# A bias table filled by copies on GpSimd instead of one-hot products on TensorE

## The chip, the cores and the metric

The kernel runs on one core of one Trainium2 chip. The metric is the device time of one execution in microseconds (us). A core has five engines with a queue of instructions each: TensorE (PE in the profile; its weight loads, PEld, overlap the products), VectorE (DVE), ScalarE (ACT), GpSimd (POOL) and SyncE (SP), which here issues nearly all transfers. An engine takes its queue in order; engines wait for each other and for transfers through semaphores.

## The reference

It is a two-layer encoder over 256 tokens of width 1024, in float32. Each layer has a mixer and a gated MLP with a width-3 convolution. The mixer projects the normed input to a pooling branch, to queries, keys and values of 12 heads, and to two gates. The heads form three groups with (window, dilation) of (128, 1), (512, 4) and (2048, 16). What matters here is the bias on the logits:

```
half = window // (2 * dilation)
buckets = _t5_buckets(dilation * np.arange(-half, half + 1))
bias = rel_bias[buckets][:, hs].T            # rel_bias: (32 buckets, 12 heads)
logits = logits + bias[None, :, None, :]
logits = where(valid, logits, NEG_INF)
```

So the bias of a query and a key depends on their distance, through one of 32 buckets, and on the head. Keys outside the window, or off the dilation's grid, are masked. Both layers use the same table.

## The kernel before

Tokens are kept as two interleaved halves (even and odd, `t`), 128 each, on the partitions. Float32 products are made of three reduced products of a high and a low part (`wh`, `wl`, made of each weight by a ScalarE cast, L177 or L185, and a VectorE subtraction, L178 or L186).

The class `Weights` streams all weights in order. `load` (L109, transfer at L117) fetches raw tiles of 1 MB through three buffers; each raw tile is cut into two pieces; a piece is split into `wh` and `wl` some three pieces ahead of its use (`get`, L194, with `LOOK` 3 and five buffers). A projection (`proj`, L479) takes one piece: eight products with 512 columns at L475 and eight with 256 columns at L477.

Layer 0 begins with the values of the first head group (`begin_values_of_x`, L582), in an order written out by hand, and the other two groups (`first_values`, L704, products at L734). After that come `load_params` (L339), the bias table, and then the eight projections of the pooling branch (L793 to L801), two for each window, then queries and keys, with the attention steps put among them.

Outside the part ordered by hand, the framework plans the order of each engine's instructions itself: it runs the program against its own costs and puts an instruction into its engine's queue when its inputs are expected to be there, in program order where several are ready. Transfers on SP are therefore not all in program order. `tc.issue_after(W.behind[1].ins)` puts what is traced inside it behind one VectorE instruction, for the instructions on that same engine only.

The bias table: for each of five kinds (distance parity and dilation) and each of 4 heads of a group there are 256 places along the distance. `_bias_table` (L54) is made on the host: rows 0 to 31 are one-hot over the buckets, row 32 holds the mask (NEG where the distance is invalid, 0 elsewhere). `load_bias` (L354) fetches it (33 x 1280) into the tag `ybig` and `rel_bias` with a row of ones below it, and splits `rel_bias` into `rh` and `rl`; ScalarE casts the table into the tag `m2`. `build_bias` (L368) is a generator: for each kind it makes two products (L374) into PSUM and a VectorE copy (L378) into `fsb`, in the tag `q1`; it is moved on by one kind before each pooling projection (L800). After the fifth, `fsb` (4 x 1280) goes to DRAM (`fd`, L383), from there 128 times over to `sk` (2.5 MB, L385), and five skewed reads (L390) make `bt`, in which the place of a query and a key is aligned. `scores` adds `bt` to the logits (L878).

The tags are single buffers with several users in turn. `m2` first holds the pieces of the first value weights, later `po2` (L943). `q1` holds `xul` (the low part of the raw input) through the values, later the queries `q`. `ybig` holds pieces of the first values, later `pl2`.

Of the kernel before, what the change touches and what calls it, by code (L numbers as in the profile page):

```python
# [10 lines left out]
F32 = mybir.dt.float32  # L11
F32R = mybir.dt.float32r
# [4 lines left out]
P = 128  # L17
# [5 lines left out]
HPG = 4  # L23
NG = 3
NH = HPG * NG
# [8 lines left out]
NT = 5  # L34
# [10 lines left out]
def _buckets(rel):  # L45
    n = -rel
    ret = (n < 0).astype(np.int32) * 16
    n = np.abs(n)
    large = 8 + (np.log(np.maximum(n, 1) / 8) / np.log(1024 / 8) * 8).astype(np.int32)
    large = np.minimum(large, 15)  # L50
    return (ret + np.where(n < 8, n, large)).astype(np.int32)


def _bias_table():  # L54

    t = np.zeros((33, NT, 256), np.float32)
    delta = np.arange(255) - 127
    for n, (e, dil) in enumerate(
        ((2 * delta, 1), (2 * delta + 1, 1), (2 * delta - 1, 1), (2 * delta, 4), (2 * delta, 16))
    ):  # L60
        valid = (e % dil == 0) & (np.abs(e) <= 64 * dil)
        b = _buckets(e)
        j = np.nonzero(valid)[0]
        t[b[j], n, j] = 1.0
        t[32, n, np.nonzero(~valid)[0]] = NEG
        t[32, n, 255] = NEG
    return t.reshape(33, NT * 256)


def _edge_table():  # L70
# [134 lines left out]
def encoder(ctx, tc, x, w_in, w_pool, pool_scale, w_a, w_b, w_o, norm1, norm2, w_up, conv_w,  # L205
            conv_b, w_down, rel_bias, norm_f, onehot, edges, out):
    nc = tc.nc
    const = ctx.enter_context(tc.tile_pool(name="const", bufs=1))
    wpool = ctx.enter_context(tc.tile_pool(name="weights", bufs=1))
    big = ctx.enter_context(tc.tile_pool(name="big", bufs=1))  # L210
    sm = ctx.enter_context(tc.tile_pool(name="small", bufs=2))
    acc = ctx.enter_context(tc.tile_pool(name="acc", bufs=4, space=bass.MemoryType.PSUM))
# [6 lines left out]
    def cols(w, c0):  # L219

        src = w[:, c0 : c0 + 256].rearrange("(k p) c -> p k c", p=P)
        return W.add(
            src, (8, 256), [((lambda t, j=j: t[:, :, j * P : (j + 1) * P]), (8, P)) for j in (0, 1)]
        )
# [10 lines left out]
    for l in range(DEPTH):  # L235
        for g in range(NG):
            c0 = C_V + g * 512
            slots = (("m2", 0, 2), ("m2", 1, 2), ("ybig",), ("at2",)) if g == 0 else ()
            for j in range(2):
                tag = "k1" if l == 0 and g == 1 and j == 0 else None  # L240
# [34 lines left out]
        for f in range(0, NF, 2):  # L275
            a = cols(w_up[l], f * P) if f >= ENTRY else []
            g = cols(w_up[l], DFF + f * P)
# [7 lines left out]
    h = const.tile([P, 2, D], F32, name="h")  # L285
# [53 lines left out]
    def load_params():  # L339

        nc.sync.dma_start(out=edge.rearrange("p a b -> p (a b)"), in_=edges[0].partition_broadcast(P))
        for l in range(DEPTH):
            rowst = sm.tile([96, P], F32, tag="s", name="prow")
            nc.sync.dma_start(out=rowst[0:66, :], in_=conv_w[l].rearrange("w (f p) -> (w f) p", p=P))
            nc.sync.dma_start(out=rowst[66:88, :], in_=conv_b[l].rearrange("(f p) -> f p", p=P))
            nc.sync.dma_start(out=rowst[88:96, :], in_=pool_scale[l].rearrange("(f p) -> f p", p=P))
            pt = mmp.tile([P, 512], F32, tag="mm", name="prm_ps")
            nc.tensor.transpose(pt[:, :96], rowst, ident[:96, :96])
            nc.vector.tensor_copy(prm[:, l, :], pt[:, :96])
            nc.vector.tensor_scalar_mul(hps[:, l, :], prm[:, l, 88:96], 0.5)  # L350

    bt = const.tile([P, HPG, NT * P], F32, name="bt")

    def load_bias():  # L354
        oh = big.tile([33, NT * 256], F32, tag="ybig", name="onehot_sb")
        nc.sync.dma_start(out=oh, in_=onehot)
        rb = sm.tile([33, NH], F32, tag="rb", bufs=1, name="rb")
        nc.vector.memset(rb, 1.0)
        nc.sync.dma_start(out=rb[0:32, :], in_=rel_bias)
        rh = sm.tile([33, NH], F32R, tag="ms", name="rh")  # L360
        rl = sm.tile([33, NH], F32R, tag="ms", name="rl")
        nc.vector.tensor_copy(rh, rb)
        nc.vector.tensor_sub(out=rl, in0=rb, in1=rh.bitcast(F32))
        ohr = big.tile([33, NT * 256], F32R, tag="m2", name="onehot_r")
        nc.scalar.copy(out=ohr, in_=oh)
        return rh, rl, ohr

    def build_bias(rh, rl, ohr):  # L368

        fsb = big.tile([HPG, NT * 256], F32, tag="q1", name="fsb")  # L370
        for n, g in enumerate((0, 0, 0, 1, 2)):
            ps = acc.tile([P, 512], F32, tag="acc", name="f_ps")
            for j, r in enumerate((rh, rl)):
                nc.tensor.matmul(  # L374
                    ps[:HPG, :256], r[:, g * HPG : (g + 1) * HPG], ohr[:, n * 256 : (n + 1) * 256],
                    start=(j == 0), stop=(j == 1),
                )
            nc.vector.tensor_copy(fsb[:, n * 256 : (n + 1) * 256], ps[:HPG, :256])  # L378
            yield

        n = HPG * NT * 256
        fd = dram.tile([1, n], F32, name="fd")
        nc.sync.dma_start(out=fd[0].rearrange("(h e) -> h e", h=HPG), in_=fsb)  # L383
        sk = dram.tile([P, n + 1], F32, name="sk")
        nc.sync.dma_start(out=sk[:, 0:n], in_=fd[0].partition_broadcast(P))  # L385
        for blk, kind in enumerate((2, 0, 1, 3, 4)):
            src = bass.AP(
                sk.tensor, sk.offset + kind * 256 + 127, [[n, P], [NT * 256, HPG], [1, P]]
            )
            nc.sync.dma_start(out=bt[:, :, blk * P : (blk + 1) * P], in_=src)  # L390
        yield

    def bias_of(t, hh):

# [96 lines left out]
    def in_order(a):  # L491

        return a.rearrange("p (m t) -> p t m", t=2)
# [70 lines left out]
    def v_tile():  # L564
        return acc.tile([P, 512], F32, tag="acc", name="v_ps")
# [176 lines left out]
    for l in range(DEPTH):  # L742
# [25 lines left out]
        else:  # L768
            for g in range(NG):
                held = begun[0] if g == 0 else [W.get() for _ in range(4)]  # L770
                for t in range(2):
                    if g + t == 0:
                        ps = begun[1]
                    else:
                        ps = v_tile()
# [6 lines left out]
        if l == 0:  # L782
            load_params()
            with tc.issue_after(W.behind[1].ins):
                bias = build_bias(*load_bias())
        g2 = gain(norm2[l])


# [4 lines left out]
        for gi in range(3, -1, -1):  # L793
            w = WINDOWS[gi]
            u = sm.tile([P, 2, S + 2 * PAD], F32, tag="u", name="u")
            nc.vector.memset(u[:, :, 0:PAD], 0.0)
            nc.vector.memset(u[:, :, PAD + S :], 0.0)
            for j in range(2):
                if l == 0:
                    next(bias, None)  # L800
                add_up(in_order(u[:, j, PAD : PAD + S]), [halves(a) for a in proj(x2)])  # L801
            cur, n = u, S + 2 * PAD
            sh = 1
            while sh < w:
                nxt = sm.tile([P, 2, S + 2 * PAD], F32, tag="us", name="us")
                n -= sh
                nc.vector.tensor_add(
                    out=nxt[:, :, 0:n], in0=cur[:, :, 0:n], in1=cur[:, :, sh : sh + n]
                )
                cur = nxt  # L810
                sh *= 2
            hw = w // 2
            o = PAD - hw
            e = edge[:, gi, 0:hw].unsqueeze(1).to_broadcast([P, 2, hw])
            nc.vector.tensor_mul(out=cur[:, :, o : o + hw], in0=cur[:, :, o : o + hw], in1=e)
            if hw > 1:
                e = edge[:, gi, hw : w - 1].unsqueeze(1).to_broadcast([P, 2, hw - 1])
                r = slice(o + S - hw + 1, o + S)
                nc.vector.tensor_mul(out=cur[:, :, r], in0=cur[:, :, r], in1=e)
            pd = sm.tile([P, 2, S], F32, tag="us", name="pd")  # L820
            nc.vector.scalar_tensor_tensor(
                out=pd, in0=cur[:, :, o : o + S], scalar=1.0 / w, in1=u[:, :, PAD : PAD + S],
                op0=ALU.mult, op1=ALU.subtract,
            )
            both = pl2[gi // 2][:, gi % 2 * 2 : gi % 2 * 2 + 2]
            ph, pl = both[:, :, 0], both[:, :, 1]
            pd = pd.rearrange("p k (m t) -> p k t m", t=2)
            nc.scalar.copy(out=ph, in_=pd)
            nc.vector.tensor_sub(out=pl, in0=pd, in1=ph.bitcast(F32))
            pooled[gi] = both  # L830
# [100 lines left out]
        for pair in ((0, 1), (2, 3)):  # L931
            a, b = pair
# [8 lines left out]
        for m, c in enumerate(PAIRS):  # L941
# [7 lines left out]
            for n in range(4):  # L949
# [5 lines left out]
                if hd < HPG:  # L955
# [3 lines left out]
                        out=lo[:, hd], in0=src, scalar=scale, in1=hi[:, hd].bitcast(F32),  # L959
# [3 lines left out]
                        out=lo[:, hd], in0=rest, scalar=scale, in1=lo[:, hd].bitcast(F32),  # L963
                        op0=ALU.mult, op1=ALU.add,
                    )
                else:
# [3 lines left out]
                        out=o, in0=src, scalar=scale, in1=o, op0=ALU.mult, op1=ALU.add  # L970
# [20 lines left out]
        for c in range(KD):  # L991
            th = gate(c)
            nc.vector.scalar_tensor_tensor(
                out=pa[:, c, :], in0=th, scalar=1.0, in1=pa[:, c, :], op0=ALU.add, op1=ALU.mult
            )
        m2 = big.tile([P, 2, KD, 2, P], F32R, tag="m2", name="m2")
        mh, ml = m2[:, 0], m2[:, 1]
        for c4 in range(2):
            ths = [gate(4 * c4 + j) for j in range(4)]
            for j2 in range(2):  # L1000
                i, (wh, wl) = W.get()
                for j in range(2):
                    c = 4 * c4 + 2 * j2 + j
                    ps = mmp.tile([P, 2, S], F32, tag="mm", name="b_ps")
# [5 lines left out]
                        out=m, in0=ths[2 * j2 + j], scalar=1.0, in1=m, op0=ALU.add, op1=ALU.mult  # L1010
# [49 lines left out]
        held, ps = entry  # L1060
        first = keep_entry(ps)
        ps = v_tile()
# [106 lines left out]
```

## Time and profile before

| what | us |
|---|---|
| median of three runs | 881.99 (881.4 to 882.06) |
| the profiled execution | 882.08 |
| its span | 880.3 |
| PE busy | 872.4 |
| DVE busy | 682.5 |
| ACT busy | 525.6 |
| POOL busy | 14.0 in 40 instructions |

The span is what the profile covers; 1.78 us of the execution lie around it. A busy share is an average over the whole run. In a timeline the first number is the start in us from the span's start, the second the length, then engine, line, operation, output and inputs, shape and count; in brackets the idle time of the engine before it and what ended it. SPq marks the issue of a transfer, not the transfer. PE's granted clock was 0.999 of full speed.

### The profile page before, as it was taken

The numbers are of one execution on the slowest core, as the hardware profiler recorded it, in microseconds if no ns is written. First come the engines' busy times: TensorE is split into PE (matmuls) and PEld (weight loads), VectorE is DVE, ScalarE is ACT, GpSimd is POOL, SyncE is SP. The second block draws the span as 40 slices with busy tenths as digits, with TensorE's granted clock in tenths as the row PEclk, the third lists the DMA queues.
The fourth block names the chain that finished last, engine by engine and source line by source line (L and its number), as shares of the span: only waits on it lengthen the run. The fifth ranks groups of instructions, "written<-read, shape, count | busy, mean of one in ns | idle before, by whom it ended". The sixth has DMA issues, their size and how long they took to land.

```text
span 880.3 us, 12800 instructions
## 1 busy us (share of the span) xinstructions
PE 872.4 (99%) x4817; PEld 757.5 (86%) x4817; DVE 682.5 (78%) x1167; ACT 525.6 (60%) x929; POOL 14.0 (2%) x40
## 2 busy tenths in 40 slices
PE   9999999999999999999999999999999999999996
PEld 7888889988888888888888888999888888888885
DVE  6988886767869987787755987776678698878774
ACT  6746654556648766666545574554566486666652
POOL 2000000000000000000000000000000000000000
PEclk9999999999999999999999999999999999999999
DMA  9669744455554665465636465443556447566541
GB/s 327 233 204 313 240 144 147 141 181 176 175 207 147 205 225 193 155 221 198 239 120 220 163 199 185 148 163 124 191 189 205 159 146 257 167 197 205 172 144 50
DMA packets 125791, 164.48 MB, mean 187 GB/s; under 512 B 2995, under 2 KB 106107, under 8 KB 125600
## 3 DMA queue, kind: packets, MB, share of 16 engines
q1 hardware_dynamic: 125712, 163.65, 56.0%
q8 instruction: 38, 0.62, 0.3%
q14 instruction: 25, 0.20, 0.1%
q10 hardware_dynamic: 16, 0.00, 0.0%
HBM read 162.57 MB, written 3.69 MB: 189 GB/s over the span
## 4 chain that ended last, share of the span: by engine, by line
PE 99%; ACT 0%; POOL 0%; DVE 0%; issue 0%; POOLq 0%; ACTq 0%
PE proj_ps L475 40%; PE proj_ps L477 21%; PE res_ps L502 6%; PE v_ps L572 6%; PE res_ps L503 6%; PE res_ps L504 6%; PE v_ps L734 2%; PE b_ps L475 2%; PE v_ps L647 1%; PE b_ps L477 1%; PE pool_ps L475 1%; PE o_ps L922 1%; PE s_ps L872 1%; PE pt_ps L901 1%; PE s_ps L867 1%; PE o_ps L918 1%
## 5 line engine op out<-in xcount | busy, mean ns | idle before, releaser
L178 DVE TENSOR_TENSOR wl<-raw,wh 128x1024 fp32r<-128x1024 f32 x274 | 334.2, 1223 | 132.8 <-ACT wh L177 128.2
L177 ACT CAST wh<-raw 128x1024 fp32r<-128x1024 f32 x274 | 286.0, 1049 | 189.4 <-PE proj_ps L475 128.4
L475 PE MATMUL proj_ps<-x,wh 128*128 128x512 f32 x1408 | 354.1, 393 | 0.0
L475 PEld LDWEIGHTS proj_ps<-x,wh 128*128 128x128 f32 x1408 | 254.1, 189 | 47.3 <-issue 0.5
L477 PEld LDWEIGHTS proj_ps<-x,wl 128*128 128x128 f32 x1408 | 192.0, 190 | 13.8
L477 PE MATMUL proj_ps<-x,wl 128*128 128x256 f32 x1408 | 196.3, 282 | 0.0
L502 PE MATMUL res_ps<-wh,actq 128*128 128x512 f32 (+1 forms) x184 | 70.2, 381 | 0.0
L503 PE MATMUL res_ps<-wl,actq 128*128 128x512 f32 (+1 forms) x184 | 70.1, 381 | 0.0
L504 PE MATMUL res_ps<-wh,actk 128*128 128x512 f32 (+1 forms) x184 | 69.9, 380 | 0.0
L504 PEld LDWEIGHTS res_ps<-wh,actk 128*128 128x128 f32 x184 | 34.6, 188 | 6.7
L502 PEld LDWEIGHTS res_ps<-wh,actq 128*128 128x128 f32 x184 | 34.7, 188 | 6.2
L503 PEld LDWEIGHTS res_ps<-wl,actq 128*128 128x128 f32 x184 | 34.7, 188 | 6.0
L475 PE MATMUL proj_ps<-po,wh 128*128 128x512 f32 x128 | 33.1, 400 | 0.0
L1099 ACT ACTIVATE y<-y 128x256 f32<-128x256 f32 x44 | 18.3, 416 | 24.7 <-DVE y L1096 24.5
L1082 ACT ACTIVATE y<-a,prm 128x256 f32<-128x256 f32 x36 | 21.6, 600 | 15.9 <-DVE a L498 15.9
L416 ACT ACTIVATE junk<-h 128x512 f32<-128x512 f32 (+1 forms) x20 | 10.9, 546 | 27.0 <-DVE h L414 27.0
L502 PE MATMUL res_ps<-wh,m 128*128 128x512 f32 (+1 forms) x72 | 26.5, 368 | 0.0
L475 PEld LDWEIGHTS proj_ps<-po,wh 128*128 128x128 f32 x128 | 22.9, 189 | 4.1
L503 PE MATMUL res_ps<-wl,m 128*128 128x512 f32 (+1 forms) x72 | 26.3, 366 | 0.0
L504 PE MATMUL res_ps<-wh,m 128*128 128x512 f32 (+1 forms) x72 | 26.3, 365 | 0.0
L572 PE MATMUL v_ps<-wh,x 128*128 128x512 f32 x80 | 25.7, 392 | 0.0
L1083 DVE SCALAR_TENSOR_TENSOR y<-a,prm,y 128x255 f32<-128x255 f32 x36 | 17.3, 480 | 8.1 <-ACT y L1082 8.1
(208 smaller groups left out, 1101.6 us busy)
## 6 DMA issues: line engine op xcount, KB each, us to landing
raw<-in_w_in_dram SPq DMA_DIRECT2D x58, 1024.0 KB, 5.7
raw<-in_w_up_dram SPq DMA_DIRECT2D x44, 1024.0 KB, 4.9
raw<-in_w_down_dram SPq DMA_DIRECT2D x22, 1024.0 KB, 4.7
raw<-in_w_a_dram SPq DMA_DIRECT2D x8, 1024.0 KB, 5.3
raw<-in_w_o_dram SPq DMA_DIRECT2D x8, 1024.0 KB, 4.9
raw<-in_w_b_dram SPq DMA_DIRECT2D x4, 1024.0 KB
sk<-fd SPq DMA_DIRECT2D x1, 2560.0 KB
raw<-in_w_pool_dram SPq DMA_DIRECT2D x2, 1024.0 KB
```

The costliest lines, as they stand in the source:

```text
L177: lambda: nc.scalar.copy(out=h, in_=src),
L178: lambda: nc.vector.tensor_sub(out=l, in0=src, in1=h.bitcast(F32)),
L475: nc.tensor.matmul(ps, wh(k), x2[:, k], start=(k == 0), stop=False)
L477: nc.tensor.matmul(ps[:, 1], wl(k), x2[:, k, 0], start=False, stop=(k == nk - 1))
L502: nc.tensor.matmul(ps, ah, wh, start=first, stop=False)
L503: nc.tensor.matmul(ps, ah, wl, start=False, stop=False)
L504: nc.tensor.matmul(ps, al, wh, start=False, stop=last)
L572: nc.tensor.matmul(ps, x2[:, 2 * n + j, part, t, :], w[:, j, :], start=(n + m == 0), stop=(n == 3 and m == 5),)
L734: nc.tensor.matmul(ps[t], a[:, k, t, :], w[:, j, :], start=(k + m == 0), stop=(k == KD - 1 and m == 2),)
L1082: nc.scalar.activation(y, a, AF.Identity, bias=b, scale=w1)
L1083: nc.vector.scalar_tensor_tensor(out=y[:, 1:], in0=a[:, : S - 1], scalar=w0, in1=y[:, 1:], op0=ALU.mult, op1=ALU.add)
L1099: nc.scalar.activation(y2, y2, AF.Tanh, scale=c)
```

## The change

The one-hot products, their operands and the generator go. `build_bias` is now an ordinary function, called once, before the pooling projections. It fetches `rel_bias` turned, one transfer for each head group, so that a head's 32 values lie along one partition; and the mask's row (row 32 of the same host table) onto four partitions of `fsb`, which is now in the tag `m2`. Then GpSimd writes each bucket's value over the places of that bucket: within one kind these are evenly spaced, so one copy from a broadcast element serves one run. There are 15, 16, 15 and 11 runs for the kinds 0, 1, 3 and 4; kind 2 is kind 1 shifted by one place, one copy of 128. That makes 58 copies. The rest, `fd`, `sk` and `bt`, is as before. The call stays inside `issue_after`, which now finds no VectorE instruction.

```
+def _runs(n):
+    t = _bias_table()[:32].reshape(32, NT, 256)[:, n]
+    runs = []
+    for b in range(32):
+        places = np.nonzero(t[b])[0]
+        if len(places):
+            step = int(places[1] - places[0]) if len(places) > 1 else 1
+            assert (np.diff(places) == step).all()
+            runs.append((b, int(places[0]), len(places), step))
+    return runs
...
-    def load_bias():
-        oh = big.tile([33, NT * 256], F32, tag="ybig", name="onehot_sb")
-        nc.sync.dma_start(out=oh, in_=onehot)
-        rb = sm.tile([33, NH], F32, tag="rb", bufs=1, name="rb")
-        nc.vector.memset(rb, 1.0)
-        nc.sync.dma_start(out=rb[0:32, :], in_=rel_bias)
...
-        nc.vector.tensor_copy(rh, rb)
-        nc.vector.tensor_sub(out=rl, in0=rb, in1=rh.bitcast(F32))
-        ohr = big.tile([33, NT * 256], F32R, tag="m2", name="onehot_r")
-        nc.scalar.copy(out=ohr, in_=oh)
...
-        fsb = big.tile([HPG, NT * 256], F32, tag="q1", name="fsb")
-        for n, g in enumerate((0, 0, 0, 1, 2)):
...
-                nc.tensor.matmul(
...
-            nc.vector.tensor_copy(fsb[:, n * 256 : (n + 1) * 256], ps[:HPG, :256])
-            yield
+    def build_bias():
+        rbt = sm.tile([HPG, NG, 32], F32, tag="rb", bufs=1, name="rbt")
+        fsb = big.tile([HPG, NT, 256], F32, tag="m2", name="fsb")
+        for g in range(NG):
...
+                nc.sync.dma_start(
+                    out=rbt[:, g], in_=rel_bias[:, g * HPG : (g + 1) * HPG].rearrange("b h -> h b")
+                )
+        nc.sync.dma_start(
+            out=fsb.rearrange("p a b -> p (a b)"), in_=onehot[32].partition_broadcast(HPG)
+        )
+        for n, g in ((0, 0), (1, 0), (3, 1), (4, 2)):
+            for b, j, count, step in _runs(n):
+                nc.gpsimd.tensor_copy(
+                    fsb[:, n, j : j + (count - 1) * step + 1 : step],
+                    rbt[:, g, b : b + 1].to_broadcast([HPG, count]),
+                )
+        nc.gpsimd.tensor_copy(fsb[:, 2, 64:192], fsb[:, 1, 63:191])
+        fsb = fsb.rearrange("p a b -> p (a b)")
...
-                bias = build_bias(*load_bias())
+                build_bias()
...
-                if l == 0:
-                    next(bias, None)
```

## The prediction

> **What bounds the kernel now.** I read the page first: busy times, then the chain that ended last.
>
> ```profile
> PE 872.4 (99%) x4817; PEld 757.5 (86%) x4817; DVE 682.5 (78%) x1167; ACT 525.6 (60%) x929; POOL 14.0 (2%) x40
> ...
> PE 99%; ACT 0%; POOL 0%; DVE 0%; issue 0%; POOLq 0%; ACTq 0%
> ```
>
> TensorE is the chain, from end to end. The list of who waited for whom, for PE alone, has two entries, 1.0 and 0.2 us. So a microsecond taken from PE's queue should come off the end, and work on another engine costs nothing until PE has to wait for it. Next, the timeline of PE where the bias table is made:
>
> ```profile
> 49.15 0.28 PE L374 MATMUL f_ps<-onehot_r,rh 33*4 33x256 f32 x1
> 49.27 0.28 PE L374 MATMUL f_ps<-onehot_r,rl 33*4 33x256 f32 x1
> 49.47 2.11 PE L475 MATMUL proj_ps<-x,wh 128*128 128x512 f32 x8
> 51.43 1.11 PE L477 MATMUL proj_ps<-x,wl 128*128 128x256 f32 x8
> 52.47 0.28 PE L374 MATMUL f_ps<-onehot_r,rh 33*4 33x256 f32 x1
> ...
> 59.01 2.00 PE L475 MATMUL proj_ps<-x,wh 128*128 128x512 f32 x8
> 60.85 1.11 PE L477 MATMUL proj_ps<-x,wl 128*128 128x256 f32 x8
> 61.80 2.00 PE L475 MATMUL proj_ps<-x,wh 128*128 128x512 f32 x8
> ```
>
> The first columns are start and length. A projection with two one-hot products beside it takes 3.32 us from start to start (49.47 to 52.79 in the same timeline), one without takes 2.79 (59.01 to 61.80). Then the queue that issues the transfers (SP), since the table goes out and back through DRAM on it, between the weight loads:
>
> ```profile
> 34.44 0.37 SPq L117 DMA_DIRECT2D raw<-in_w_in_dram  x1
> ...
> 57.68 0.27 SPq L383 DMA_DIRECT2D fd<-fsb  x1
> 61.28 0.59 SPq L385 DMA_DIRECT2D sk<-fd  x1
> 64.68 0.39 SPq L117 DMA_DIRECT2D raw<-in_w_in_dram  x1
> 72.81 3.79 SPq L390 DMA_DIRECT2D bt<-sk  x5
> 76.69 28.95 SPq L117 DMA_DIRECT2D raw<-in_w_in_dram  x8
> ```
>
> From the write of fd to the fifth bt transfer are 18 us; SP stands in that time and a weight load waits behind it, yet PE does not wait. The first reader of bt is at 113.87 (DVE L878). Last, what POOL's small instructions cost, alone and beside VectorE:
>
> ```profile
> 250.58 0.22 POOL L423 TENSOR_SCALAR ss<-ss 128x1 f32<-128x1 f32 x1 [232.03 <-ACT junk L416]
> ...
> 436.17 0.63 POOL L423 TENSOR_SCALAR ss<-ss 128x1 f32<-128x1 f32 x1 [176.49 <-ACT junk L416]
> 438.29 0.19 POOL L425 TENSOR_TENSOR ss<-ss 128x1 f32<-128x1 f32 x1 [1.49 <-ACT junk L416]
> ```
> ```profile
> 435.50 1.23 DVE L178 TENSOR_TENSOR wl<-raw,wh 128x1024 fp32r<-128x1024 f32 x1 [0.77 <-ACT wh L177]
> ```
>
> The same instruction takes 0.22 us, and 0.63 when a VectorE subtraction with two SBUF inputs is running, ending as that one ends; the subtraction keeps its length (1.22 us is the mean of 274).
>
> **The change, part by part.** Base: the profiled execution, 882.08 us (span 880.3 and 1.78 around it); the median shown is 881.99, so 0.09 comes off at the end.
>
> Removed from PE: ten products. Five projections start between 42.37 and 56.11, and the sixth at 59.01: 16.64 us for five, against 5 x 2.795 without products (the two steps from 59.01 to 64.60). The difference, 2.66 us, is the price with every gap around the products in it (one of them 0.35 us of waiting for rl). All of it is on the chain.
>
> Removed elsewhere: ScalarE's cast of the one-hot table (1.26 us at 27.23), VectorE's five copies (0.405 each), memset, cast and subtraction (0.07, 0.16, 0.16). That is 3.7 us off the path, since PE waits for neither engine there; I count nothing. If it shortened waits of PE, there are 1.2 us of those in the whole span, most of it before 1.04: at most a few tenths.
>
> Added on SP: three transfers of rel_bias, turned (128 elements of 4 bytes each), and the mask's row onto four partitions, in place of onehot and rb (0.29 and 0.33 us to issue). No row has a transfer of single elements; bounds are 0.27 (fd) and 0.98 (the longest bt issue), so four cost 1.1 to 3.9 us; I take 0.4 each, near the median of small ones. They belong around 20.5, where onehot was issued; SP idles from 21.23 to 24.59, which hides the excess of 1 to 3.3 us. If that cover went, the next weight load (24.59, cast at 33.13) still has over 2 us to spare after a landing of 5.7.
>
> Added on POOL: 57 copies of one bucket's run (15, 16, 15 and 11 for the four tables, as the bucket function gives them) and one of 128 elements. No row is a POOL copy. Bounds: 0.10 us (MEMSET, 128x1) and 0.63 (the row above); I take 0.2, because the instructions of one column that read SBUF (0.19 and 0.22) are nearest. POOL is otherwise idle from 18.54 to 250.58, so nothing queues behind the copies there; the wait they add is on SP, at fd.
>
> When are they done? They need the mask and the three pieces. The tag m2, where fsb now lies, is free after the last product that reads it (14.75); with issue around 20.5 and about 3.5 us to land (fd was followed by sk, which waited for it, 3.6 us later) they start at 24. From 24 to 47 VectorE runs 18 instructions with two SBUF inputs (4 L722, 8 L186, 6 L178: 16.0 us). That leaves 7 us, or 35 copies, plus one at each of the 18 boundaries (as POOL's L623 at 16.89, which ended at 17.53 between two L186): 53 of 58 by 47, all by about 47.5. With 0.10 each it is about 38; with 0.63 each, 60.5. Before, the table was ready at 57.6. Even at 60.5, fd to landed bt (23.5 us) gives 84, and the reader comes at 111. The next user of m2 (po2, first written near 79) also finds it free. So, by itself, the table is early enough.
>
> A rule of the Trainium skill (GPSIMD Engine Reference, "Instruction dispatch") speaks against this start: the first call of a freshly loaded POOL kernel costs about 6 us more and shows no instruction. The rows show nothing so long: POOL's first TENSOR_SCALAR pair, at 10.98, took 2.00 us in all. By the rule the copies would end near 53.5, which leaves the sum as it is.
>
> Sum: 882.08 - 2.66 = 879.42; against the median 879.3 us, or 0.30% faster. A measurement here tells about 0.2% (1.8 us) from nothing.
>
> **The rivals.** First, slower: SP stands at fd too early. Each engine's order is planned ahead, so SP's queue has fd where the plan expects the copies to be done; the plan need not know that VectorE holds POOL up. SP takes its entries in order. If fd is put ahead of the weight load at 34.44, the load goes only when the last copy is done. That load's first piece is cast at 39.74, 5.3 us after its issue, and read by the third projection, which after the change starts at 42.37 + 2 x 2.79 = 47.96; with 1.05 us for the cast it must be issued by 41.6. Copies done at 47.5 are 0.3 + 5.9 = 6.2 us too late: 879.3 + 6.2 = 885.5. The point that decides is a last copy after 41.6 together with that place in the queue; at 38 nothing is lost, at 60.5 it is 19 us (898). For it: rb was issued at 38.24, out of program order, so the plan does move transfers, and copies of 0.2 us look cheap to a plan. Against it: before, the plan put fd where its wait was 1.2 us, and the later loads have more room (37.08 to a use at 53.6: issue by 47.2).
>
> Second, no change: VectorE pays. In 24 to 37 VectorE prepares the second and third group's weights just ahead of PE. If each of its 12 instructions with two SBUF inputs there waited for a copy in progress, that is 12 x 0.2 = 2.4 us on the path: 881.7. Against it: where POOL's first instructions came in, from 10.98, the neighbouring VectorE instructions still follow each other without a gap (L186 at 9.09 for 2.08, L616 at 11.09, L630 at 11.70). The Trainium skill (SBUF — State Buffer, "Who interferes with whom") has a rule by which this would happen: a VectorE instruction with two SBUF inputs and a POOL instruction that reads SBUF exclude each other, and whichever comes second waits. The trace agrees for POOL as the second (0.63 against 0.22 us); no row shows VectorE as the second.
>
> That the change does not do what it says is hardly possible: the ten products are gone from the program.
>
> **How the numbers follow.** The gain with the wait hidden: 0.60. VectorE pays: 0.14. SP stands too early: 0.26, from 0.4 for that place in the queue and 0.65 for copies that end after 41.6. The forecast is the first, 879.3, with its own range of 878.4 (a few tenths of waits saved, and the spread of the runs) to 880.2. The range reaches to the price of the first rival, 885.5; its half above that (0.13) and some 0.05 below are left out. Faster by over 0.2%: 0.58 from the forecast, 0.02 from each rival, 0.62. Same: 0.02, 0.09 and 0.04, 0.15. Slower: 0.03 and 0.20, 0.23.
>
> **What would show it.** Right: no L374 group; projections from 42 on 2.79 us apart; POOL copies of 0.1 to 0.3 us ending between 38 and 50, some stretched to the end of a VectorE subtraction; PE's waits still near 1.2 us; bt landed well before 111. Wrong by the first rival: SP waits long at fd for POOL, the loads after it are issued in a bunch, and PE or ScalarE waits for a raw tile in 45 to 65. Wrong by the second: L186 or L178 longer than 0.75 and 1.23 us, or gaps before them, and PE waiting for wl before 42.

## The result: 1.35% slower

The changed kernel takes 893.9 us (median of 4, 893.44 to 894.27) against 882.02 for the kernel before: a ratio of 1.0135, 95% interval 1.0123 to 1.0147. The profiled execution took 893.98 us with a span of 892.2. The page of the changed kernel, busy times and the chain:

```profile
PE 870.8 (98%) x4807; PEld 757.5 (85%) x4807; DVE 680.2 (76%) x1159; ACT 525.7 (59%) x928; POOL 29.1 (3%) x98
...
PE 92%; DMA 4%; POOL 2%; SPq 0%; ACT 0%; issue 0%; DVE 0%; POOLq 0%; ACTq 0%
```

PE has less work than before (870.8 us for 872.4, ten products fewer), but the chain is no longer PE alone: a transfer and GpSimd stand in it. The list of who waited for whom, PE only (us in total, times, longest), has one new entry:

```profile
PE proj_ps L484 <- ACT wh L190: 13.4, 1, 13.4
PE gain_ps L346 <- DVE ones L332: 1.0, 1, 1.0
```

PE's timeline shows the place: the third projection of the pooling branch. (Line numbers have moved: L484 and L486 are the products that were L475 and L477.)

```profile
41.75 2.07 PE L484 MATMUL proj_ps<-x,wh 128*128 128x512 f32 x8
43.65 1.12 PE L486 MATMUL proj_ps<-x,wl 128*128 128x256 f32 x8
44.61 2.00 PE L484 MATMUL proj_ps<-x,wh 128*128 128x512 f32 x8
...
60.94 3.53 PE L484 MATMUL proj_ps<-x,wh 128*128 128x512 f32 x8 [13.38 <-ACT wh L190]
64.30 1.11 PE L486 MATMUL proj_ps<-x,wl 128*128 128x256 f32 x8
65.25 2.00 PE L484 MATMUL proj_ps<-x,wh 128*128 128x512 f32 x8
```

It should have begun at 47.40 (44.61 + 2.79). What held it is in the chain of the changed kernel, here in order of time (start, us, what):

```profile
27.03 14.94 POOL fsb L383 x57
41.97 0.23 POOL fsb L388
...
42.22 1.97 DMA fd<-fsb
...
44.20 0.58 SPq L395
...
44.89 14.85 DMA raw<-in_w_in_dram
...
59.84 1.05 ACT wh L190
...
60.94 3.53 PE proj_ps L484 x8
```

GpSimd finishes the table at 42.2; SP has stood at fd for it (15.3 us in the list of SP's waits), with the weight load behind. The load goes out at 44.89, where the kernel before issued it at 34.44, and then needs 14.85 us to land, and 14.95 us to its first cast, which came 5.3 us after the issue before. The two effects, the later issue and the longer way, are 10.5 and 9.6 us. The slack of that load absorbs a part, and 13.4 us of waiting remain.

The account: +13.4 for the wait; +1.5, because the third projection takes 4.31 us to the next one (60.94 to 65.25) and not 2.79; -2.66 for the products; -0.6, because the first projection already starts 0.62 us earlier (41.75 for 42.37). That is 11.6 of the 11.9 us between the spans. The 1.5 us are a lower granted clock after the pause (stretches of the changed kernel; after the busy times of PE, PEld, DVE, ACT and POOL comes the clock):

```profile
58.00:61.00 3.00, 0.07 (x1) 0.07 (x1) 0.08 (x1) 1.16 (x2) 0.00 (x0) 0.50 1.09 383
61.00:63.00 2.00, 2.00 (x5) 1.61 (x6) 2.00 (x2) 1.58 (x4) 0.00 (x0) 0.50 1.14 349
63.00:65.00 2.00, 2.00 (x11) 1.68 (x10) 1.97 (x5) 1.83 (x2) 0.00 (x0) 0.74 1.13 343
65.00:67.00 2.00, 2.00 (x12) 1.71 (x11) 2.00 (x3) 0.39 (x1) 0.00 (x0) 1.00 1.09 381
```

The clock is at half when PE starts again, and full 3.1 us later (at 64.03); half of that time is lost, which is the 1.5 us. The Trainium skill (TensorE: Matmul & The Clock Gate, "The HAM clock gate") describes this gate, with about 3.4 us of sustained work to open it. The rows agree roughly: in the three kernels below that also pause, PE starts again 2.8, 4.0 and 5.0 us before the clock is full for good.

### The profile page after: what moved, and what is told of

Same layout as the page of the kernel before. It is cut to its first block, busy times and chain, and to the rows that moved or that the text cites. A ratio compares the mean times of both kernels' runs of the same rounds, so it can differ in the third digit from the quotient of the medians.

```text
span 892.2 us, 12835 instructions
## 1 busy us (share of the span) xinstructions
PE 870.8 (98%) x4807; PEld 757.5 (85%) x4807; DVE 680.2 (76%) x1159; ACT 525.7 (59%) x928; POOL 29.1 (3%) x98
## 4 chain that ended last, share of the span: by engine, by line
PE 92%; DMA 4%; POOL 2%; SPq 0%; ACT 0%; issue 0%; DVE 0%; POOLq 0%; ACTq 0%
PE proj_ps L484 39%; PE proj_ps L486 20%; PE res_ps L511 6%; PE v_ps L581 6%; PE res_ps L512 6%; PE res_ps L513 6%; DMA raw<-in_w_in_dram 3%; POOL fsb L383 2%; PE b_ps L484 2%; PE b_ps L486 1%; PE pool_ps L484 1%; PE o_ps L929 1%; PE s_ps L879 1%; PE pt_ps L908 1%; PE s_ps L874 1%; PE o_ps L925 1%
## 5 line engine op out<-in xcount | busy, mean ns | idle before, releaser
L191 DVE TENSOR_TENSOR wl<-raw,wh 128x1024 fp32r<-128x1024 f32 x274 | 334.4, 1223 | 147.0 <-ACT wh L190 144.4
L484 PE MATMUL proj_ps<-x,wh 128*128 128x512 f32 x1408 | 354.9, 394 | 13.4 <-ACT wh L190 13.4
L484 PEld LDWEIGHTS proj_ps<-x,wh 128*128 128x128 f32 x1408 | 255.2, 189 | 60.1 <-ACT wh L190 13.6
L486 PEld LDWEIGHTS proj_ps<-x,wl 128*128 128x128 f32 x1408 | 192.0, 190 | 13.8
L486 PE MATMUL proj_ps<-x,wl 128*128 128x256 f32 x1408 | 196.3, 282 | 0.0
L484 PE MATMUL proj_ps<-po,wh 128*128 128x512 f32 x128 | 33.1, 400 | 0.0
L432 POOL TENSOR_SCALAR ss<-ss 128x1 f32<-128x1 f32 x8 | 2.2, 274 | 820.1 <-ACT junk L425 820.1
L484 PEld LDWEIGHTS proj_ps<-po,wh 128*128 128x128 f32 x128 | 22.9, 189 | 4.1
```

What stands on the lines that cost most here:

```text
L191: lambda: nc.vector.tensor_sub(out=l, in0=src, in1=h.bitcast(F32)),
L484: nc.tensor.matmul(ps, wh(k), x2[:, k], start=(k == 0), stop=False)
L486: nc.tensor.matmul(ps[:, 1], wl(k), x2[:, k, 0], start=False, stop=(k == nk - 1))
```

## The experiments

Theory after the result: two things made the load late, SP standing at fd, and sk, issued just ahead of it, whose 2.5 MB the load's data have to wait for or share with. The rivals: the standing alone; sk's traffic alone, on any queue; the copies slowing VectorE.

**The products alone.** The kernel before, without its ten products.

```
-            ps = acc.tile([P, 512], F32, tag="acc", name="f_ps")
-            for j, r in enumerate((rh, rl)):
-                nc.tensor.matmul(
-                    ps[:HPG, :256], r[:, g * HPG : (g + 1) * HPG], ohr[:, n * 256 : (n + 1) * 256],
-                    start=(j == 0), stop=(j == 1),
-                )
-            nc.vector.tensor_copy(fsb[:, n * 256 : (n + 1) * 256], ps[:HPG, :256])
+            nc.vector.tensor_copy(
+                fsb[:, n * 256 : (n + 1) * 256],
+                ohr[:HPG, n * 256 : (n + 1) * 256].bitcast(F32),
+            )
```

> The kernel before, with the ten one-hot products left out and the copies to fsb reading the cast table instead, so the bias is wrong. Nothing moves to GpSimd. Theory: the products' own price is the 2.66 us read from the spacing of the projections: 879.3 us, between 878.8 and 879.9. Rival (the products fill time that PE would have waited): within 1 us of the kernel before.

Measured: 879.14 us against 881.51, ratio 0.9969 (0.9957 to 0.9981). From the second on, all projections are 2.79 us apart (the first takes 2.86), as in its timeline:

```profile
47.82 2.00 PE L472 MATMUL proj_ps<-x,wh 128*128 128x512 f32 x8
49.66 1.11 PE L474 MATMUL proj_ps<-x,wl 128*128 128x256 f32 x8
50.61 2.00 PE L472 MATMUL proj_ps<-x,wh 128*128 128x512 f32 x8
```

So the gain was sized rightly: 0.31% by the ratio (2.4 us between the medians, 2.75 between the profiled spans) where 0.30% was forecast. The change removes the same products.

**sk behind the loads.** In the changed kernel, only sk and bt are queued later.

```
         nc.sync.dma_start(out=fd[0].rearrange("(h e) -> h e", h=HPG), in_=fsb)
+        yield
         sk = dram.tile([P, n + 1], F32, name="sk")
...
-                build_bias()
+                export = build_bias()
+                next(export)
...
+                sums = proj(x2)
+                if l == 0 and export and 8 in W.issued:
+                    with tc.issue_after(W.issued[8].ins):
+                        next(export, None)
+                    export = None
...
```

`W.issued[8]` is the transfer of the ninth weight load, which feeds the fifth projection.

> The copies and fd stay where the change put them; only sk and bt are queued on SP behind the weight load that feeds the fifth projection. Theory (the late load came from two things: SP stood at fd until 42.2, and then the load's data queued behind the 2.5 MB of sk and took 14.9 us to land): the load is issued near 43 and lands in about 6 us, PE waits 2 to 3 us instead of 13.4, time 880 to 883 us. Rival (the wait of SP at fd is the whole loss, sk ahead of the load does not matter): the load still lands near 58, PE waits 11 us or more, time above 890.

Measured: 886.31 us, ratio 1.0053 (1.004 to 1.0066). SP in this run, then pieces of its chain and PE's third projection:

```profile
42.06 0.26 SPq L393 DMA_DIRECT2D fd<-fsb  x1
42.37 0.36 SPq L303 DMA_DIRECT2D gain<-in_norm_dram  x1
42.83 4.46 SPq L130 DMA_DIRECT2D raw<-in_w_in_dram  x3
47.39 2.72 SPq L396 DMA_DIRECT2D sk<-fd  x1
```
```profile
42.83 7.07 DMA raw<-in_w_in_dram
...
51.08 2.36 DVE wl L191 x2
53.44 0.18 DVE prm L362
```
```profile
53.75 3.75 PE L485 MATMUL proj_ps<-x,wh 128*128 128x512 f32 x8 [5.35 <-DVE prm L362]
```

The load lands in 7.07 us (with the 512 KB of gain just ahead of it), at 49.90 and not at 59.74, and the kernel is 7.6 us faster than the change. So sk ahead of the load was about half of the loss (14.8 us, from the 879.14 of the products alone to 893.9), and the rival that the standing is all of it falls. The time is still above the 880 to 883 expected. The wait was 5.3 us and not 2 to 3, and the low clock cost 2.4 us more (53.75 to 58.93 for one projection). The late load also stopped VectorE at its subtractions, and behind them stood the copy of prm (conv and pooling parameters) that empties one of the four PSUM buffers which the projections use too; PE's row names that copy as what it waited for. Here a late load is dearer than its own lateness, because VectorE, too, takes its queue in order.

**The copies' end, moved.** Three versions of the changed kernel leave SP's order up to the table alone and move only the time at which GpSimd is done: no copies, the 32 of kinds 0 to 2, and the 57 runs done twice.

```
-        for n, g in ((0, 0), (1, 0), (3, 1), (4, 2)):
+        for n, g in ((0, 0), (1, 0)):
...
+        for n, g in ((0, 0), (1, 0), (3, 1), (4, 2)) * 2:
```

The first new line is that of the half table, the second that of the table done twice; without copies, the loop and the copy of 128 places go.

> The changed kernel with all 58 copies left out: fsb holds the mask alone, and fd, sk and bt go at the same places of SP's queue. Theory (the place is harmless when fsb is ready where the plan expects it): fd goes near 27, sk's data are through by 40, before the third projection's load is needed, PE does not wait, 878.5 to 880 us. Rival (sk ahead of the load costs several us in any case): PE waits 3 us or more, 883 us or more.

> The changed kernel with the runs of kinds 3 and 4 left out (32 copies instead of 58), so those parts of the bias stay at the mask's 0; SP's queue has the same order. Theory (the third projection's load goes after fd and sk and lands some 14 us after its issue, because 3 MB are ahead of it): the copies end between 35.5 and 39.5, the load is issued 2.5 us later and lands near 53 to 57, PE waits 7 to 11 us and loses 1.5 us more by a low clock; 887 to 891 us. Rival (the prediction's rule: copies that end before 41.6 cost nothing): under 880.5 us.

> The changed kernel with the 57 copies of runs done twice over (115 in all, the result is the same). Theory (nothing covers a later end, so each us of it goes to the end): the second half runs while VectorE is idle, 57 copies of 0.18 us, the copies end near 52.3, and the time is 10.4 us above the changed kernel: 903 to 906 us. Rival (PE's wait comes from sk's 2.5 MB and not from the copies): within 3 us of the changed kernel.

| us | copies end | sk issued | load issued | load landed | third projection | median | ratio |
|---|---|---|---|---|---|---|---|
| no copies | - | 28.90 | 34.10 | 44.7 | 47.44 | 879.27 | 0.9966 (0.9953 to 0.9979) |
| half | 32.3 | 34.29 | 34.97 | 50.7 | 51.92 | 885.68 | 1.0051 (1.0031 to 1.007) |
| the change | 42.2 | 44.20 | 44.89 | 59.7 | 60.94 | 893.9 | 1.0135 |
| twice | 47.7 | 49.73 | 50.41 | 66.1 | 67.33 | 900.78 | 1.0218 (1.0202 to 1.0233) |

The half table is the plainest row. Its SP queue, the load in its chain, and PE's third projection:

```profile
32.30 0.27 SPq L393 DMA_DIRECT2D fd<-fsb  x1
32.62 0.36 SPq L303 DMA_DIRECT2D gain<-in_norm_dram  x1
34.29 0.58 SPq L395 DMA_DIRECT2D sk<-fd  x1
34.97 5.72 SPq L130 DMA_DIRECT2D raw<-in_w_in_dram  x2
```
```profile
34.97 15.76 DMA raw<-in_w_in_dram
```
```profile
51.92 3.28 PE L484 MATMUL proj_ps<-x,wh 128*128 128x512 f32 x8 [4.38 <-ACT wh L190]
```

The load is issued at its usual time, SP has hardly stood, and yet it lands 15.76 us later and PE waits 4.4 us (plus 1.7 by the clock: 4.46 us to the next projection). So sk ahead is enough for a loss, without the standing. Over the four rows the load lands 15.8, 16.4, 15.5 and 16.4 us after the issue of sk, whenever the load itself was issued. The records of the transfers' packets show why. In the changed kernel, from 46 to 53 us:

```profile
DMA packets 97, 1.99 MB, mean 284 GB/s; under 512 B 0, under 2 KB 0, under 8 KB 0
```

These are sk's packets of 20 KB alone. The load was issued at 44.89, but its packets, of 1 KB, begin only after 53, when 109 of sk's 128 have begun. So on this queue the load waits for sk. That is the rule the prediction lacked: with this order, sk's issue plus 16 us plus 1.1 for the cast is the third projection's earliest start. It was due at 47.40, so sk must be issued by about 30.3, and the copies must end by about 28. Without copies sk goes at 28.90 and nothing is lost. The change ends them at 42.2, and 44.2 + 16 + 1.1 - 47.4 = 13.9, against 13.4 measured.

The numbers expected for half and twice were missed (887 to 891 and 903 to 906). In both the copies started 2 us earlier than in the changed kernel's profile (24.95 and 24.70, not 27.03: the mask landed earlier). In half they then also missed the worst of VectorE's stretch; in twice the second 57 copies took 7.1 us and not 10.3, because copies begin 0.125 us after one another, though each lasts 0.18. From the change to twice the table ends 5.5 us later and the time grows by 6.9.

**Another queue.** Only fd, sk and bt move, from SP to GpSimd's own queue (five `nc.sync.dma_start` become `nc.gpsimd.dma_start`).

> Only the queue of fd, sk and bt is changed, from SP to GpSimd, which made the copies and has nothing else to do until 250 us. Theory: the wait for the copies stands on a queue that nobody needs, the load that feeds the third projection is issued near 34 again, PE waits about 1.2 us in all, 878.5 to 880.5 us. Rival (the 2.5 MB of sk in 42 to 55 us delay the weights, on whatever queue they are issued): some later load lands more than 10 us after its issue, PE waits several us, 883 us or more.

Measured: 879.94 us (878.26 to 883.95), ratio 0.9984 (0.9972 to 0.9997), with more spread than any other. SP issues the load at 34.90. GpSimd's timeline shows the same waits as SP's before, with nobody behind them:

```profile
41.71 0.76 POOL L393 DMA_DIRECT2D fd<-fsb  x1 [0.31 <-POOL fsb L388]
46.63 0.58 POOL L395 DMA_DIRECT2D sk<-fd  x1 [4.16 <-DMA fd<-fsb]
58.98 3.76 POOL L400 DMA_DIRECT2D bt<-sk  x5 [11.77 <-DMA sk<-fd]
```

sk's traffic lies in the same stretch of time, and the profiled run's PE waits 2.2 us in all, so the rival's price did not come. Half of its mechanism did, though. The loads issued before sk (34.90 to 43.74) land within 5.1 to 6.4 us. The one issued just behind it, at 47.04, is cast only at 61.27:

```profile
47.04 0.37 SPq L130 DMA_DIRECT2D raw<-in_w_in_dram  x1
```
```profile
61.27 1.05 ACT L190 CAST wh<-raw 128x1024 fp32r<-128x1024 f32 x1 [3.49 <-DMA raw<-in_w_in_dram]
```

Between 49 and 57 GpSimd's queue (q0) moves 20 times as many bytes as SP's (q1), on which that load is waiting:

```profile
q0 software_dynamic: 114, 2.27, 92.5%
q1 hardware_dynamic: 105, 0.11, 8.2%
```

So sk holds loads up from another queue as well. It costs nothing here because the loads that were due next had gone out ahead of sk; the one held up feeds the eleventh projection counted from 42, which starts at 70.60. Two of the twelve runs took over 883 us; whether that is this traffic was not followed up.

**The export where it was.** Copies as in the change; fd, sk and bt are traced after the sixth of the loads that follow the values and queued behind it, with the same means as in the second experiment (`yield` ahead of fd, `W.issued[11]`).

> Copies as in the change; fd, sk and bt are queued on SP behind the sixth pair of pooling and query weights, about where the kernel before had them. Theory: SP does not stand while weights are due, PE's waits are back near 1.2 us, and the removed products show: 878.5 to 880 us, faster than both kernels. Rival (the copies on GpSimd themselves slow VectorE or the weights): no faster than 881.5.

Measured: 879.4 us (878.46 to 879.87), ratio 0.997 (0.9958 to 0.9982). SP and the waits of PE:

```profile
34.11 12.48 SPq L130 DMA_DIRECT2D raw<-in_w_in_dram  x5
46.68 0.43 SPq L394 DMA_DIRECT2D fd<-fsb  x1
51.99 0.37 SPq L130 DMA_DIRECT2D raw<-in_w_pool_dram  x1
52.45 0.58 SPq L396 DMA_DIRECT2D sk<-fd  x1
```
```profile
PE gain_ps L346 <- DVE ones L332: 1.0, 1, 1.0
PE proj_ps L485 <- DVE po L860: 0.6, 1, 0.6
...
```

PE waits 2.2 us in all, where 1.2 was expected. This is the version with the whole table that most clearly beats both kernels. It has all 58 copies on GpSimd and gains as much as the two versions in which GpSimd copies nothing (0.9969 and 0.9966), so the copies cost nothing that can be measured, and the third rival falls too.

## Why the prediction was wrong

The forecast, 879.3 us, was the case "the gain with the wait hidden", and the time came out 8 us above the range. Its first rival happened, with its place (fd ahead of the load that feeds the third projection) and its kind (SP stands, that load is late). The step that failed is this rival's price and the point from which it decides: "it must be issued by 41.6". By that rule, copies that end at 42.2 lose about 1 us, and the half table loses nothing; they lost 13.4 and 4.4 us of PE's time, and the low clock on top, for which the price had no term. The rule took the load's own 5.3 us to its cast as fixed. But sk was now issued just ahead of it, and with sk ahead the load lands 16 us after sk's issue. The sum has the same hole: it has no term for fd, sk and bt at their new place.

The trace before had this price. sk was issued at 61.28, and bt waited for it until 72.81, 11.5 us in which the transfer engines were busy for 0.85 of the time. The weight load issued next, at 64.68, was cast 15.4 us after sk's issue:

```profile
76.65 2.95 ACT L177 CAST wh<-raw 128x1024 fp32r<-128x1024 f32 x3 [0.30 <-DMA raw<-in_w_in_dram]
```

The prediction counted these 18 us as harmless, because PE had not waited; it did not ask which load would stand behind sk at the new place, nor when that load was due.

The chance of 0.26 followed from the same mistake. A last copy after 41.6 was given 0.65, but the true limit is near 28, and hardly any time for the copies would have met it: 58 copies 0.125 us apart with none held up, started at 24.7, the earliest start in any run, would end near 32 (an estimate from these rows); the half table ended at 32.3 and lost. Once fd stood ahead of that load in the queue, to which 0.4 was given, a loss was all but sure.

Point by point:

- The products' price, 2.66 us: right (0.31% in the experiment). The engines' other removed work, counted at nothing: PE's waits show no gain from it; the first projection starts 0.62 us earlier, but in two variants of the same kernel (sk behind the loads, another queue) it starts 0.2 us later than before, so this is no steady gain, and its cause is not shown.
- The four new transfers: three of rel_bias took 1.10 us to issue and the mask 0.30, 1.4 us for the 1.6 estimated, and the load after them was issued at 23.95, earlier than before.
- The copies: 0.18 us each when free (median 182 ns), 0.125 us from start to start, for 0.2 taken. They started at 27.03, not 24, and ended at 42.2, not 47.5: the lower price helped, and so did the late load itself, which left VectorE idle from 38.98. Where that load was on time (the export where it was), the copies started at 25.4 and ended at 43.4.
- "One at each boundary" between VectorE's instructions was half right. The stretches of the changed kernel, with POOL's count in the fifth bracket (an instruction that crosses an edge is counted on both sides):

```profile
30.00:33.00 3.00, 3.00 (x14) 2.45 (x14) 3.00 (x6) 3.00 (x5) 3.00 (x15) 1.00 0.02 5
33.00:36.00 3.00, 3.00 (x15) 2.47 (x14) 3.00 (x6) 1.33 (x2) 3.00 (x5) 1.00 0.00 0
36.00:39.00 3.00, 3.00 (x15) 2.49 (x14) 2.98 (x4) 0.69 (x1) 3.00 (x3) 1.00 0.00 0
39.00:42.00 3.00, 3.00 (x16) 2.48 (x15) 0.08 (x1) 0.16 (x1) 3.00 (x25) 1.00 0.00 0
```

  VectorE's weight subtractions run back to back from 32.66 to 38.98, six of 0.74 us (L199) and two of 1.22 (L191). At each of the five boundaries between those of L199 one copy gets in; at the two beside L191 none does, and one copy lasts 2.99 us, from 36.03 to 39.02. So 6 copies begin in the six us from 33 to 39, and 23 in the three us after.
- VectorE as the one that waits: no. Its subtractions keep their lengths in the changed kernel (L199 0.736 to 0.749 us, L191 1.203 to 1.228; before, 0.741 to 0.748 and 1.202 to 1.228), and the gain is whole with all copies in place. The rule of the Trainium skill that whichever comes second waits (SBUF — State Buffer, "Who interferes with whom") was seen for GpSimd alone.
- The 6 us of a first call (Trainium skill, GPSIMD Engine Reference, "Instruction dispatch"): the trace does not show them; the first copy starts 0.12 us after the mask has landed (26.91), and GpSimd finished 6 copies within 1.04 us of that start.
- What was to show the first rival did: a long wait of SP at fd for GpSimd, loads issued in a bunch, ScalarE waiting for raw (17.3 us) between 42 and 60. The wait on the table itself was, as predicted, no matter: the last part of bt landed at 66.2, and its first reader came at 125.7.

## What to carry to other kernels

When a step moves to an idle engine, look at the queue that waits for its end: what stands behind that wait, when it is due, and which large transfer will now go out just ahead of it. Price the transfer's bytes as well as the wait; here a load issued on time behind 2.5 MB landed as long after that transfer's issue as one issued 10 us later. A planned order holds for the plan's durations, so pin a transfer that depends on a slow or disturbed engine behind the loads that are due first. A queue that nobody needs takes away the wait for the engine, but not the transfer's traffic.

## What was not expected of the hardware

- With a 2.5 MB DRAM-to-DRAM transfer issued ahead on the same queue, a 1 MB load landed 15.5 to 16.4 us after that transfer's issue in four kernels, although it was issued 0.7 to 5.2 us after it. Its packets hardly begin before the other's are through. On another queue the same transfer still held a load up: 14.2 us from issue to cast, where loads issued before it landed in 5.1 to 6.4.
- A GpSimd copy that reads SBUF can be held through several VectorE instructions with two SBUF inputs, not only to the end of one: 2.99 us for one that takes 0.18 when free, in all five kernels that make the copies of kinds 3 and 4. Between back-to-back instructions of 0.74 us one copy did get in each time.
- A pause of PE of 4.4 us is already followed by 1.7 us of loss to the lower clock, more than a third on top of the wait. Longer pauses did not cost more in step: 2.4 us after 5.3, 1.5 after 13.4, 1.4 after 19.8.
